# Turning the neighbourhood attention's probabilities: six TensorE transpositions a head replaced by VectorE block transpositions and a trip through DRAM

## The chip, the cores and the metric

The kernel runs on one core of one Trainium2 chip. The core has five engines that each work through their own instruction list in order and wait for one another by semaphores: TensorE (PE in the profile; PEld is its loading of stationary operands), VectorE (DVE), ScalarE (ACT), GpSimd (POOL) and SyncE (SP), which here issues nearly all transfers. The metric is device time in microseconds (us) of one launch, lower is better. A single core is used, so there is nothing to balance between cores.

## The reference, cut to what matters

The program is a two-layer encoder over 512 grid tokens and 16 learned "meta" tokens, 1024 features wide. In each layer one normalised input is projected to 42 chunks of 128 columns. They feed two attention branches and their gates; both branches are projected back, weighted by sigmoid gates, added and projected once more to the residual stream.

```python
# branch A: 8 query heads on 2 key heads, every query sees all 528 keys
p = softmax(q @ k.T * scale); o = p @ v
# branch B (neighbourhood): 8 heads, a grid query sees a window of 8 x 16 grid neighbours
# (with a learned bias) and the 16 meta keys; a meta query sees the meta keys alone
s_win  = einsum('bchd,bicjhd->bhcij', q_row, k_win) * scale + bias
s_meta = einsum('bchd,bmhd->bhcm', q_row, km) * scale
p = softmax(concat([s_win, s_meta])); o = p_win @ v_win + p_meta @ vm
```

All of it is float32. TensorE multiplies float32 values that were split into a high and a low part, and a product is the sum of three matmuls (high by high, high by low, low by high).

The second product of attention needs the probabilities with keys on the partitions (the 128 rows of on-chip memory), while the softmax leaves queries on them. So every block of probabilities has to be transposed between the two. That step is what the change is about.

## The kernel before, in words

The spine is `product` (line 316): one chunk of weights by all tokens. In layer 0 it runs two spans of 264 tokens with 24 matmuls each; in layer 1, where meta tokens are needed for keys and values alone, most chunks run one span of 512. Weights come in halves of 256 KB. `weights` (line 231) issues the load of a half on SP into one of four `raw` buffers, three halves ahead of their use; ScalarE then casts the high part (`whi`, line 240) and GpSimd subtracts the low part (`wlo`, line 241). So each weight load sits in SP's list among all other transfers, and a transfer that has to wait on SP holds up the weight loads behind it.

Attention is woven into the spine. After each span (and in the middle of a 512 span in layer 1) `tick` (line 310) is called, and two `Side` objects (line 279), one for each branch, run the parts that fall due. A unit of work starts every four ticks, and its parts have fixed numbers of ticks after the start: `GQA_AT` and `NA_AT` (lines 37 to 40). The neighbourhood branch starts one tick after the other (`GQA_AT_TICK, NA_AT_TICK`, line 44). A planner then orders each engine's list by the order in which the code was traced and its own estimates of readiness; parts under `high_priority` are drawn ahead.

`windowed_head` (line 967) is one head of the neighbourhood branch. Eight run in a layer. Its parts are:

- `prepare` (tick 0): SP loads the bias table (480 KB) into a `bias` tile of 960 columns; there are two such tiles.
- `scores` (tick 2): the queries are four tiles of 128, and each needs 208 or 272 keys (`BLK`, four column ranges of the bias tile). TensorE writes scores, VectorE adds the bias and takes the row maximum (line 990), ScalarE takes the exponential in place (line 992). In layer 0 there are 16 meta queries beside.
- `transposes1`, `transposes2`, `transposes3` (ticks 5, 5, 5 in layer 0; 4, 5, 5 in layer 1): nine TensorE transpositions (line 129, `transposed`) into three PSUM banks named `ta`, `tb`, `tc`: six of 128 by 128 probabilities, two of 80 columns (the tokens that only an edge tile needs with the meta keys), one of 64 columns around the meta keys. In layer 0 a fourth bank `tm` takes the meta queries. All come from the pool `ps_t`, which has two banks. `split` (line 191) empties a bank: ScalarE copies the high part (line 193), VectorE subtracts the low part (line 194). `split_meta` (line 784) does so for the meta keys.
- `sums` (tick 7): eleven matmuls with the values (line 1052) into one bank `avb`; then `combine` (line 765) and, after the second head of a pair, `gated` (line 775) write `ob`, the branch's output.

Beside them `divided_later` (line 800) sends the row sums of a pair of heads through DRAM and multiplies their inverse into the gate `zb` on GpSimd (line 822); it too has its transfers on SP. After the last head `side_na.finish()` runs all parts that are left with no ticks between, and the branch's output projection (`y<-ob`) follows.

Branch A (`global_unit`, line 847) already turns its probabilities another way, and its lines are a measure here: VectorE transposes within blocks of 32 by 32 in place (line 867), SP writes the tile to DRAM (line 870, `turn<-P`), reads it back in four transfers that put the blocks in their places (line 877, `P<-turn`), and `split` works from on-chip memory (`pth`, `ptl`).

## Time and profile before

| | |
|---|---|
| time, median of 3 runs | 853.73 us (852.26 to 855.82) |
| the profiled execution's own time | 855.46 us |
| its span, first to last instruction | 853.1 us |
| granted TensorE clock, mean | 0.992 |
| busy PE / PEld / DVE / ACT / POOL | 97% / 89% / 65% / 56% / 45% |
| neighbourhood heads run, layer 0 and layer 1 | about 84 to 256 us and 505 to 672 us |
| transfers | 135 MB in 113249 packets, mean 158 GB/s |

How to read it: the matmuls overlap, and a line's mean duration runs from its start to its modelled end, so the rate of the engine is read from the distance between starts. "Idle before" is time in which the engine stood still ahead of a group of instructions, and the arrow names what ended that time. The granted clock is 1.00 or 0.50 in any short stretch.

### The profile page before, as it was taken

To read this page: it belongs to the slowest core of one execution; us is meant where nothing else is said; L and a number is where in the kernel's file an instruction comes from. 1 tells how busy PE (TensorE), PEld (TensorE's weight loads), DVE (VectorE), ACT (ScalarE), POOL (GpSimd) and SP (SyncE) were. 2 spreads that over 40 slices of the span, in tenths; PEclk is the share of its full clock that TensorE was granted. 3 is DMA by queue.
4 is the path that set the end of the run, shared out by engine and by line. 5 is a ranking of instruction groups with operands and counts; after the bars stand their busy time and mean duration, and the time that the engine had idled before them with its cause. 6 is when DMAs were issued, how large, how long until landed. Compare 5 with 4: busy or idle time off the path is not lost.

```text
span 853.1 us, 16107 instructions
## 1 busy us (share of the span) xinstructions
PE 825.1 (97%) x5662; PEld 762.1 (89%) x5662; DVE 552.0 (65%) x1218; ACT 473.7 (56%) x1137; POOL 382.6 (45%) x296
## 2 busy tenths in 40 slices
PE   9999899989999999899999999999999999999997
PEld 9999899989999999899998989898987778878786
DVE  7976658777776675436447657777777657555633
ACT  8654677566764555333435456576757645543422
POOL 1663343343343333545765554443534433445851
PEclk9999999999999999999999999999999999999999
DMA  7277464566544564334555575657476655544502
GB/s 275 90 194 215 122 183 122 172 205 169 169 139 137 164 184 145 112 100 144 147 143 130 142 212 161 170 165 238 124 206 172 193 163 169 169 151 145 176 13 99
DMA packets 113249, 135.00 MB, mean 158 GB/s; under 512 B 31888, under 2 KB 66192, under 8 KB 113168
## 3 DMA queue, kind: packets, MB, share of 16 engines
q1 hardware_dynamic: 112448, 132.90, 53.0%
q8 instruction: 45, 0.74, 0.4%
q10 hardware_dynamic: 720, 1.06, 0.3%
q14 instruction: 36, 0.29, 0.1%
HBM read 98.50 MB, written 21.84 MB: 141 GB/s over the span
## 4 chain that ended last, share of the span: by engine, by line
PE 78%; DVE 8%; ACT 6%; issue 4%; DMA 2%; SPq 1%; POOL 1%; POOLq 0%; ACTq 0%; DVEq 0%
PE pp L327 16%; PE pp L325 16%; PE pp L326 16%; PE av L905 4%; PE y L327 3%; PE y L326 3%; PE y L325 3%; PE avb L1052 2%; DVE ptl L194 2%; PE pf L1234 2%; PE pf L1236 2%; PE pf L1235 2%; PE S L556 2%; PE S L557 1%; DVE ga L898 1%
## 5 line engine op out<-in xcount | busy, mean ns | idle before, releaser
L241 POOL TENSOR_TENSOR wlo<-raw,whi 128x512 fp32r<-128x512 f32 x210 | 289.2, 1386 | 404.7 <-ACT whi L240 325.0
L325 PE MATMUL pp<-hh,whi 128*128 128x264 f32 (+3 forms) x1040 | 326.6, 314 | 2.7 <-DVE mg L1131 1.5
L327 PE MATMUL pp<-hh,wlo 128*128 128x264 f32 (+3 forms) x1040 | 326.2, 314 | 1.3 <-POOL wlo L241 1.2
L326 PE MATMUL pp<-hl,whi 128*128 128x264 f32 (+3 forms) x1040 | 324.3, 312 | 0.0
L327 PEld LDWEIGHTS pp<-hh,wlo 128*128 128x128 f32 x1040 | 196.8, 189 | 12.9 <-POOL wlo L241 2.1
L325 PEld LDWEIGHTS pp<-hh,whi 128*128 128x128 f32 x1040 | 196.5, 189 | 12.4 <-DVE mg L1131 1.7
L326 PEld LDWEIGHTS pp<-hl,whi 128*128 128x128 f32 x1040 | 197.0, 189 | 9.5
L240 ACT CAST whi<-raw 128x512 fp32r<-128x512 f32 x210 | 127.6, 618 | 109.1 <-PE pp L326 41.1
L867 DVE STREAM_TRANSPOSE P<-P 128x512 f32<-128x512 f32 x64 | 46.4, 727 | 36.4 <-ACT P L841 35.7
L194 DVE TENSOR_TENSOR ptl<-P,pth 128x512 fp32r<-128x512 f32 x64 | 53.8, 841 | 5.4 <-ACT pth L193 4.7
L837 DVE CUSTOM_DVE_ANT_1 P<-S,r 128x528 f32<-128x528 f32 x64 | 44.9, 701 | 16.0 <-PE S L557 15.1
L1131 DVE TENSOR_TENSOR mg<-pp,rbc 128x264 f32<-128x264 f32 (+1 forms) x48 | 24.8, 517 | 39.0 <-PE pp L327 38.5
L841 ACT ACTIVATE P<-P,st 128x528 f32<-128x528 f32 x64 | 47.2, 737 | 1.9
L1132 ACT ACTIVATE mg<-mg 128x264 f32<-128x264 f32 (+1 forms) x48 | 23.7, 494 | 35.0 <-DVE mg L1131 34.8
L992 ACT ACTIVATE bias<-bias,stb 128x208 f32<-128x208 f32 (+1 forms) x64 | 31.0, 486 | 20.0 <-DVE stb L990 19.9
L193 ACT CAST pth<-P 128x512 fp32r<-128x512 f32 x64 | 39.3, 614 | 0.1
L840 ACT ACTIVATE st<-st 128x1 f32<-128x1 f32 x64 | 13.0, 203 | 45.4 <-DVE st L837 44.6
L905 PE MATMUL av<-ptl,VA 128*128 128x256 f32 x128 | 34.1, 294 | 3.3 <-DVE ptl L194 3.1
L326 PE MATMUL pp<-mx,whi 128*128 128x264 f32 x128 | 36.6, 286 | 0.0
L327 PE MATMUL pp<-mx,wlo 128*128 128x264 f32 x128 | 36.4, 284 | 0.0
L325 PE MATMUL pp<-mx,whi 128*128 128x264 f32 x128 | 36.3, 284 | 0.0
L905 PE MATMUL av<-pth,VA 128*128 128x256 f32 x128 | 34.8, 295 | 0.0
(534 smaller groups left out, 1731.6 us busy)
## 6 DMA issues: line engine op xcount, KB each, us to landing
raw<-in_w_dram SPq DMA_DIRECT2D x210, 256.0 KB
turn<-P SPq DMA_DIRECT2D x32, 528.0 KB
P<-turn SPq DMA_DIRECT2D x128, 128.0 KB
bias<-in_bias_dram SPq DMA_DIRECT2D x16, 480.0 KB
KB<-KB SPq DMA_DIRECT2D x24, 272.0 KB
rawl<-in_w_dram SPq DMA_DIRECT2D x16, 256.0 KB
x<-in_xT_dram SPq DMA_DIRECT2D x8, 264.0 KB
xr<-in_xT_dram SPq DMA_DIRECT2D x8, 264.0 KB
```

Of the source, the lines that this page charges most:

```text
L193: split_at["hi"] = nc.scalar.copy(hi, src)
L194: split_at["any"] = nc.vector.tensor_sub(lo, src, hi.bitcast(F32))
L240: cast = nc.scalar.copy(hi, raw)
L241: sub = nc.gpsimd.tensor_sub(lo, raw, hi.bitcast(F32))
L325: nc.tensor.matmul(ps, wh, rh[:, a:b], start=i == 0, stop=False)
L326: nc.tensor.matmul(ps, wh, rl[:, a:b], start=False, stop=False)
L327: nc.tensor.matmul(ps, wl, rh[:, a:b], start=False, stop=i == n - 1)
L837: newest["max"] = nc.vector.tensor_tensor_reduce(p[:n].rearrange("p (i k) -> p i k", i=2), S[:n, :, :HALF], scale[:n].unsqueeze(2).to_broa ...
L841: nc.scalar.activation(p[:n], p[:n], AF.Exp, bias=st[:n, 1:2], scale=1.0, accum_out=st[:n, 2:3] if total is None else total)
L867: nc.vector.transpose(c["both"][:n, a:b], c["both"][:n, a:b])
L905: nc.tensor.matmul(c["av"], rows2(c["t"][i][0]), c["t"][i][1], start=i == 0, stop=i == 8)
L992: nc.scalar.activation(pb[b], pb[b], AF.Exp, bias=st[:, b:b + 1], scale=-1.0, accum_out=total[:, b:b + 1])
```

## The change

The six full tiles of a head's probabilities (all 128 rows of the four query tiles, columns 80 to 464 and 496 to 880 of the bias tile) are no longer transposed by TensorE. The parts become:

- `turn` (tick 3): VectorE transposes the two column ranges of 384 in blocks of 32 by 32, in place, and one transfer writes both (384 KB) to a DRAM tile `turnedb`.
- `meta_turn` (tick 4, layer 0 alone): the meta queries' transposition, formerly in `transposes1`.
- `edges` (tick 4): the three transpositions that are left go into one bank `tb`; `split` on 80 by 256 and `split_meta` empty it.
- `back` (tick 4): four transfers of 96 KB read the blocks back into columns 0 to 768 of the same bias tile, each piece 32 values (128 bytes) long.
- `split_tiles` (tick 6): the high and low parts are made from the bias tile, a 128 by 512 and a 128 by 256 split.
- `sums` (tick 7): the same eleven matmuls in another order; the output bank holds the query tiles in the order 0, 2, 1, 3, and `combine` puts them right while adding.

The bias tile is now held until tick 6 rather than tick 5. The diff, cut to its core:

```diff
--- before.py
+++ after.py
@@ -36,8 +36,8 @@
 
 GQA_AT = ({"scores": (0, 1), "turn": (1, 2), "back": 3, "split": (5, 5), "ends": 5, "divide": (3, 4, 6), "sums": (7, 7)},
           {"scores": (0, 1), "turn": (1, 2), "back": 3, "split": (5, 5), "ends": 5, "divide": (3, 4, 6), "sums": (7, 7)})
-NA_AT = ({"stages": (0, 2, 5, 5, 5, 7), "values": (3, 4), "divide": (3, 4, 6)},
-         {"stages": (0, 2, 4, 5, 5, 7), "values": (3, 4), "divide": (3, 4, 6)})
+NA_AT = ({"stages": (0, 2, 3, 4, 4, 4, 6, 7), "values": (3, 4), "divide": (3, 4, 6)},
+         {"stages": (0, 2, 3, 4, 4, 6, 7), "values": (3, 4), "divide": (3, 4, 6)})
 
 NORM_AT = ({"tokens": (0, 1, 3), "squares": (1, 1, 2, 3, 2), "heads": (2, 3, 5, 7, 6), "values": (1, 4)},
            {"tokens": (1, 3, 5), "squares": (2, 2, 2, 3, 2), "heads": (2, 3, 5, 7, 6), "values": (1, 4)})
@@ -762,7 +762,7 @@
                 nc.vector.scalar_tensor_tensor(t[:, :N], th[:, :N], 1.0, t[:, :N], op0=ALU.add, op1=ALU.mult)
             return t
 
-        def combine(tag, o, hh, av, c0, n):
+        def combine(tag, o, hh, av, c0, n, order=lambda v: v):
 
             r, q = rows(hh)
             t = slot(tag, f"cmb{nc.next_id()}")
@@ -770,7 +770,7 @@
             with ExitStack() as held:
                 if "max" in newest:
                     held.enter_context(tc.issue_after(newest["max"].ins))
-                nc.vector.tensor_add(o[r, c0:c0 + n], av[r, :n], t[r, :n])
+                nc.vector.tensor_add(o[r, c0:c0 + n], order(av[r, :n]), order(t[r, :n]))
 
         def gated(tag, o, gate, name):
             hi, lo = two(tag, name, F32R)
@@ -964,6 +964,10 @@
 
         ob, kvq, zb = [None] * 4, {}, {}
 
+        def blocks(v):
+
+            return v.rearrange("p (x y q) -> p y x q", x=2, y=2)
+
         def windowed_head(hd):
 
             j, hh, nm = hd // 2, hd % 2, f"{l}_{hd}"
@@ -1004,55 +1008,68 @@
                     nc.scalar.mul(pm, pm, sm[:, 2:3])
                     c["pm"] = pw
 
-            def transposes1():
-                pb = c["p"]
-                tp = bank(ps_t, f"ta{nm}", "tp")
-                for i, (b, o0) in enumerate(((0, 80), (1, 16), (1, 144), (2, 0))):
-                    transposed(tp[:, P * i:P * (i + 1)], pb[b][:, o0:o0 + P])
-                c["a"] = slot("B", f"tah{nm}", F32R), slot("B", f"tal{nm}", F32R)
-                split(c["a"][0][:, :512], c["a"][1][:, :512], tp)
-                if full:
-                    ps = bank(ps_t, f"tm{nm}", "tp")[:32]
-                    transposed(ps[:, :P], c["pm"])
-                    ps = ps[:, :NMETA]
-                    mh = pad_tile("mm")
-                    nc.vector.tensor_copy(mh[:32], ps)
-                    nc.vector.tensor_sub(mh[64:96], ps, mh[:32].bitcast(F32))
-                    c["mt"] = mh
-
-            def transposes2():
+
+            def turn():
+                v = c["bias"][:, EDGE:EDGE + 832].rearrange("p (s x) -> p s x", s=2)[:, :, :3 * P]
+                for s in range(2):
+                    nc.vector.transpose(v[:, s], v[:, s])
+                c["there"] = dpool.tile([P, 6 * P], F32, tag="turnedb", bufs=3, name=f"turnb{nm}")
+                nc.sync.dma_start(c["there"].rearrange("p (s x) -> p s x", s=2), v)
+
+            def meta_turn():
+                ps = bank(ps_t, f"tm{nm}", "tp")[:32]
+                transposed(ps[:, :P], c["pm"])
+                ps = ps[:, :NMETA]
+                mh = pad_tile("mm")
+                nc.vector.tensor_copy(mh[:32], ps)
+                nc.vector.tensor_sub(mh[64:96], ps, mh[:32].bitcast(F32))
+                c["mt"] = mh
+
+            def edges():
+
                 pb = c["p"]
                 tp = bank(ps_t, f"tb{nm}", "tp")
-                transposed(tp[:, 0:P], pb[2][:, P:2 * P])
-                transposed(tp[:, P:2 * P], pb[3][:, 0:P])
-                transposed(tp[:EDGE, 2 * P:3 * P], pb[0][:, :EDGE])
-                transposed(tp[:EDGE, 3 * P:4 * P], pb[3][:, P:P + EDGE])
+                transposed(tp[:EDGE, :P], pb[0][:, :EDGE])
+                transposed(tp[:EDGE, P:2 * P], pb[3][:, P:P + EDGE])
+                transposed(tp[:64, 2 * P:3 * P], c["bias"][:, BLK_META:BLK_META + 64])
                 c["b"] = bh, bl = slot("B", f"tbh{nm}", F32R), slot("B", f"tbl{nm}", F32R)
-                split(bh[:, :256], bl[:, :256], tp[:, :256])
-                split(bh[:EDGE, 256:512], bl[:EDGE, 256:512], tp[:EDGE, 256:512])
-
-            def transposes3():
-                tp = bank(ps_t, f"tc{nm}", "tp")
-                transposed(tp[:64, :P], c["bias"][:, BLK_META:BLK_META + 64])
+                split(bh[:EDGE, 256:512], bl[:EDGE, 256:512], tp[:EDGE, :256])
 
                 c["m"] = tm = pad_tile("na")
-                split_meta([(tm[:, P:2 * P], tp[:, :P]), (tm[:, :P], tp[:, :P])], inner)
+                split_meta([(tm[:, :P], tp[:, 2 * P:3 * P]), (tm[:, P:2 * P], tp[:, 2 * P:3 * P])], inner)
+
+            def back():
+
+                there = c["there"].rearrange("(b j) (s x) -> j s b x", j=32, s=6)
+                for q in range(4):
+                    nc.sync.dma_start(c["bias"][32 * q:32 * q + 32, :6 * P].rearrange("j (s b i) -> j s b i", s=6, b=4),
+                                      there[:, :, :, 32 * q:32 * q + 32])
+
+            def split_tiles():
+                v = c["bias"][:, :6 * P].rearrange("p (s t x) -> p t s x", s=2, t=3)
+                c["a"] = slot("B", f"tah{nm}", F32R), slot("B", f"tal{nm}", F32R)
+                split(*(t[:, :512].rearrange("p (t s x) -> p t s x", t=2, s=2) for t in c["a"]), v[:, :2])
+                split(*(t[:, :256].rearrange("p (s x) -> p s x", s=2) for t in c["b"]), v[:, 2])
 
             def sums():
                 VB2, o = kvq[j]["v2"], kvq[j]["o"]
                 av = bank(ps_a, f"avb{nm}", "avn")
-                seq = [(5, c["m"], 0, 128, 384)]
+
+                cols = av.rearrange("p (x y q) -> p x y q", x=2, y=2)
+                seq = [(5, c["m"], 0, av[:, 128:384])]
+                for t in c["b"]:
+                    seq += [(3, t, 256, av[:, :128]), (4, t, 384, av[:, 384:])]
                 for t in c["a"]:
-                    seq += [(0, t, 0, 0, 256), (1, t, 256, 128, 384)]
+                    seq += [(0, t, 0, cols[:, :, 0]), (1, t, 256, av[:, 128:384])]
                 for t in c["b"]:
-                    seq += [(2, t, 0, 256, 512), (3, t, 256, 0, 128), (4, t, 384, 384, 512)]
-
-                for i, (u, t, c0, a, b) in enumerate(seq):
-                    r = slice(0, EDGE if u in (3, 4) else P)
-                    nc.tensor.matmul(av[:, a:b], rows2(VB2[r, u, hh]), t[r, c0:c0 + b - a], start=i == 0,
+                    seq += [(2, t, 0, cols[:, :, 1])]
+
+                for i, (u, t, c0, out) in enumerate(seq):
+                    r, n = slice(0, EDGE if u in (3, 4) else P), P if u in (3, 4) else 2 * P
+                    nc.tensor.matmul(out, rows2(VB2[r, u, hh]), t[r, c0:c0 + n], start=i == 0,
                                      stop=i == len(seq) - 1, skip_group_check=True)
                 def collect(av=av):
-                    combine("B", o, hh, av, 0, NREAL)
+                    combine("B", o, hh, av, 0, NREAL, blocks)
                     if full:
                         combine("B", o, hh, c["avm"], NREAL, NMETA)
                     if hh == 1:
@@ -1063,7 +1080,8 @@
                     nc.tensor.matmul(c["avm"], rows2(VB2[:, 5, hh]), c["mt"], start=True, stop=True)
                 ending.append(collect)
 
-            return prepare, scores, transposes1, transposes2, transposes3, sums
+            parts = [prepare, scores, turn, edges, back, split_tiles, sums]
+            return parts[:3] + ([meta_turn] if full else []) + parts[3:]
 
 
         stacks = {"next": 0, "scored": 0}
```

## The prediction

> **What bounds the kernel now.** I read the page's engine table first, then the chain that ended last, then the groups of instructions by shape, then two windows that hold the neighbourhood heads.
>
> ```profile
> span 853.1 us, 16107 instructions
> PE 825.1 (97%) x5662; PEld 762.1 (89%) x5662; DVE 552.0 (65%) x1218; ACT 473.7 (56%) x1137; POOL 382.6 (45%) x296
> PE 78%; DVE 8%; ACT 6%; issue 4%; DMA 2%; SPq 1%; POOL 1%; POOLq 0%; ACTq 0%; DVEq 0%
> 84.00:256.00 172.00, 163.42 (x1321) 160.58 (x1320) 124.44 (x348) 114.62 (x321) 66.97 (x52) 0.98 0.56 161
> 505.00:672.00 167.00, 162.12 (x1028) 144.10 (x1027) 125.91 (x300) 112.13 (x289) 69.76 (x51) 1.00 0.61 178
> ```
>
> TensorE is busy 97% of the span and is 78% of the chain, so a matmul taken away counts in full unless something else comes late. In the two windows (window, its length, then busy PE, PEld, DVE, ACT, POOL, the granted clock, share and rate of the transfers) VectorE is busy 250 of 339 us. PE stands idle 13.5 us there, and part of that is the step being changed:
>
> ```profile
> L129 PE MATMUL tb<-ident,bias 128*128 128x128 f32 x32 | 6.4, 281 | 4.7 <-DVE mm L1020 3.3 <-DVE tal L194 1.5
> L129 PE MATMUL tc<-ident,bias 128*64 128x128 f32 x16 | 4.5, 279 | 2.4 <-DVE mm L1020 2.0 <-DVE tal L194 0.4
> 98.49 0.63 PE L129 MATMUL tb<-ident,bias 128*128 128x128 f32 x4 [3.04 <-DVE mm L1020]
> 190.96 0.27 PE L129 MATMUL tc<-ident,bias 128*64 128x128 f32 x1 [2.03 <-DVE mm L1020]
> 99.50:102.90 3.40, 3.40 (x17) 3.40 (x16) 1.53 (x4) 1.09 (x4) 0.00 (x0) 0.50 0.71 233
> 191.60:195.00 3.40, 3.40 (x19) 3.37 (x19) 2.63 (x12) 1.45 (x6) 0.00 (x0) 0.50 0.54 142
> ```
>
> In one tick four banks are asked of a pool of two, and the third transposition stands until VectorE has emptied a bank. Those waits are 4.7 + 2.4 = 7.1 us in all. The two longest are each followed by a stretch of 3.4 us with the clock at 0.50, where the matmuls take twice as long: 1.7 us lost each.
>
> **The change part by part.** Durations come from the profiled execution, whose own time is 855.46 us (span 853.1 and 2.4 around it). That lies 1.73 above the median shown, 853.73, so I sum against 855.5 and take 1.7 off at the end.
>
> *Transpositions removed.* Six a head, 96 in all. Their mean of 272 ns is a latency; the rate is read from starts:
>
> ```profile
> 94.13 0.60 PE L129 MATMUL ta<-ident,bias 128*128 128x128 f32 x4
> 94.57 0.27 PE L129 MATMUL tm<-ident,pm 128*32 128x128 f32 x1
> ```
>
> Four take 94.57 - 94.13 = 0.44 us, 0.11 each: 96 x 0.11 = **-10.6 us**. The eleven matmuls of `sums` stay as they are.
>
> *Bank waits.* After the change a head asks for `tm` and `tb` in layer 0, and `tb` alone in layer 1, in one tick. On even heads `window_values` at tick 4 asks for a third, behind `tm`. I take 1.0 of the 7.1 as left: **-6.1 us** (bounds 0, if VectorE's lateness only moves the wait elsewhere, and -7.1). With the waits go the two slow stretches: **-3.4 us** (bounds 0 and -3.4).
>
> *VectorE, ScalarE, GpSimd.*
>
> ```profile
> L194 DVE TENSOR_TENSOR ptl<-P,pth 128x512 fp32r<-128x512 f32 x64 | 53.8, 841 | 5.4 <-ACT pth L193 4.7
> L194 DVE TENSOR_TENSOR tal<-ta,tah 128x512 fp32r<-128x512 f32 x16 | 10.9, 679 | 3.0 <-ACT tah L193 2.8
> L194 DVE TENSOR_TENSOR tbl<-tb,tbh 128x256 fp32r<-128x256 f32 x16 | 6.7, 418 | 1.9 <-ACT tbh L193 1.7
> L867 DVE STREAM_TRANSPOSE P<-P 128x512 f32<-128x512 f32 x32 | 22.7, 710 | 17.4 <-ACT P L841 17.1
> L193 ACT CAST pth<-P 128x512 fp32r<-128x512 f32 x64 | 39.3, 614 | 0.1
> L193 ACT CAST tah<-ta 128x512 fp32r<-128x512 f32 x16 | 9.3, 582 | 5.3 <-PE ta L129 5.2
> L241 POOL TENSOR_TENSOR wlo<-raw,whi 128x512 fp32r<-128x512 f32 x210 | 289.2, 1386 | 404.7 <-ACT whi L240 325.0 <-PE ta L129 14.1 <-PE tc L129 9.6
> ```
>
> Per head VectorE gains two block transpositions of 128x384 (no such row; between 710 x 384/512 = 0.53 and the full 0.71; 0.53 taken, since length sets most of it) and subtractions that now read on-chip memory (0.84, and half of it, 0.42, for 128x256). It sheds 0.68 and 0.42. Net 2 x 0.53 + 0.84 + 0.42 - 0.68 - 0.42 = +1.2 us, 20 us over 16 heads, which takes VectorE from 250 to 270 of 339 us. ScalarE's copies differ by 0.03. The sum takes **0** for both: PE's work covers them. If a fifth of the 20 us shows, it is 4.
>
> The rows show the on-chip subtraction at 841 ns against 679 with one operand in PSUM. The Trainium skill (SBUF — State Buffer, Who interferes with whom) gives a reason: a VectorE instruction with two operands in SBUF shares a read port with GpSimd, and one fully blocks the other. By that rule each head's new subtractions could hold up `wlo` by up to 1.3 us (estimate: 0.84 + 0.42), 20 us of blocking in all; the sum would move only as far as GpSimd's 404.7 us of idle time did not absorb it.
>
> *Transfers and SP.* Per head five more entries in SP's list. For their price I read branch A:
>
> ```profile
> 533.84 2.72 SPq L877 DMA_DIRECT2D P<-turn  x4
> 540.83 0.62 ACT L193 CAST pth<-P 128x512 fp32r<-128x512 f32 x1
> 608.66 0.33 SPq L870 DMA_DIRECT2D turn<-P  x1
> SPq L870 <- DVE P L867: 60.1, 16, 6.9
> SPq L877 <- DMA turn<-P: 28.4, 23, 3.6
> 404.13 1.60 SPq L1197 DMA_DIRECT2D x1d<-xt  x3
> 405.40:407.30 1.90, 1.90 (x17) 1.90 (x17) 0.00 (x0) 0.62 (x1) 0.51 (x1) 1.00 0.83 156
> ```
>
> Issue is 0.33 + 2.72 = 3.05 us a head. The wait of the write for VectorE is 60.1/16 = 3.8 us where there is one, the wait of the read for the write 28.4/23 = 1.2. Behind both stand weight loads. Pieces of 128 bytes: the only rows are the `x1d` stores, three of 64 KB in such pieces, in the 1.9 us window; so 384 KB take at most 2 x 1.9 = 3.8 us, most of it while the reads are still being issued; the transfer engines, at 0.56 and 0.61 in the two windows, have room for it.
>
> How much SP has to spare shows in layer 1:
>
> ```profile
> 599.72 2.44 SPq L235 DMA_DIRECT2D raw<-in_w_dram  x2
> 619.45 0.90 SPq L235 DMA_DIRECT2D raw<-in_w_dram  x2
> 627.08 0.50 PE L327 MATMUL pp<-hh,wlo 128*128 128x512 f32 x1 [0.71 <-POOL wlo L241]
> 643.13 0.50 PE L325 MATMUL pp<-hh,whi 128*128 128x512 f32 x1 [1.08 <-ACT whi L240]
> ```
>
> From 602.2 to 619.4 no weight load leaves SP, because it stands at branch A's turn and at other waits; 7.6 us after the late load PE stands still for it. So some of SP's new 8 us a head (3.05 + 3.8 + 1.2) reaches PE. Bounds 0, if it falls where loads are early, and 8 us in each of the two holes that already show, 16. Most loads are not that late, so I take **+4 us**.
>
> *The wait of `sums` for the trip.* From the last exponential: turn 1.1, write issued 0.3, landed and read back about 1.2 + 2.7 issue, landing 2 (the row at 540.83 bounds it by 4.3), split 0.61 + 0.84 + 0.42 = 1.9. Together 9.2 us. Today's room:
>
> ```profile
> 598.19 0.45 ACT L992 ACTIVATE bias<-bias,stb 128x208 f32<-128x208 f32 x1
> 611.51 0.28 PE L1052 MATMUL avb<-na,VB 128*128 128x256 f32 x1
> L905 PE MATMUL av<-ptl,VA 128*128 128x256 f32 x128 | 34.1, 294 | 3.3 <-DVE ptl L194 3.1
> ```
>
> 611.5 - 598.6 = 12.9 us, so it fits with 3.7 to spare if SP is on time. Branch A, with the same scheme, loses 3.3 us over 32 units in PE waits for `ptl`; for 16 heads with one tick less I take **+2 us** (0 to 10).
>
> *The last head of layer 1* has no ticks left to cover it:
>
> ```profile
> 662.18 0.45 ACT L992 ACTIVATE bias<-bias,stb 128x208 f32<-128x208 f32 x1
> 669.51 0.35 PE L1052 MATMUL avb<-na,VB 128*128 128x256 f32 x1
> 675.74 1.29 POOL L822 TENSOR_TENSOR zb<-zb,sumsb 128x512 f32<-128x512 f32 x1
> 678.60 0.50 PE L325 MATMUL pp<-hh,whi 128*128 128x512 f32 x1 [1.53 <-DVE mg L1131]
> ```
>
> Exponentials to `sums` is 6.9 us today and 9.2 after. The gate `zb` is behind SP too: its read of the row sums comes after the four reads of `back`, 2.7 us. PE already waits at the end, so I take **+3 us** (0 to 8).
>
> *Sum.* -10.6 - 6.1 - 3.4 + 4 + 2 + 3 = -11.1. 855.5 - 11.1 = 844.4; less 1.7, **843 us**. The first three terms are the gain, 20.1, and the last three are what comes back, 9.
>
> **The rivals.**
> B, *nothing comes back*: SP's delays fall where weight loads are early. For it: the `wlo` row's 325 us of idle time behind `whi`, so weights are mostly ahead. Against it: the two stops at 627 and 643. 853.7 - 20.1 = 833.6; with the bounds of the small terms 831 to 837.
>
> C, *the trip is late for `sums`*. If a piece of 128 bytes costs as much as one of branch A's 512 bytes, then the 3072 pieces of a head take 3 times as long as the 1024 of the four reads at 533.84: with the 2.72 us in which those are issued, 8.2 us rather than 3.8. Then the trip is 13.6 us against 12.9, and every wait on SP shows. Eight heads of layer 1 at 1.5 us and three slow stretches of 1.7 are 17; the gain less that and the +3 at the end is 0: about 853. The Trainium skill (DMA: Bandwidth & Descriptors, Specifications) speaks for it: transfers in pieces under 512 bytes don't reach full rate. The `x1d` row speaks against so high a price, but those are stores, and these are loads.
>
> D, *SP holds the weights back*, slower. Place: weight loads behind the new write and read, in layer 1 from 560 to 650 us. Price: 8 us a head wholly exposed, and 1.7 for the slow clock after it, 9.7. It decides from two such heads on (19.4 against 20.1 gained). With three, 29 - 20 = +9: 863 us. For it: the hole at 602. Against it: SP's list has 221 us of waiting for free `raw` buffers, which shrinks before PE feels anything:
>
> ```profile
> SPq L235 <- POOL wlo L241: 221.0, 113, 7.9
> ```
>
> That the change does not do what it says would be the bank waits staying elsewhere: 9.5 of the gain gone, 853, an outcome like C's.
>
> **How the numbers follow.** The forecast (837 to 849) 0.40, B 0.18, C with the case just named 0.21, D 0.21. About 0.5%, 4.3 us, is what a measurement of this kernel can tell from no change: faster is below 849.5, slower above 858. Faster 0.40 + 0.18 = 0.58, same 0.21, slower 0.21. The range goes from B's 831 into the mild part of D, 860; outside lie about 0.03 below and 0.17 above. The forecast's own range is 837 to 849, from terms of +2 to +15 coming back instead of 9.
>
> **What would show it.** The `tb` and `tc` rows with waits of VectorE gone, x48 transpositions instead of x144, and no clock of 0.50 near 100 and 192 us: the gain. PE waits for `wlo` and `whi` over 2.7 us in all, or `raw` rows with gaps of more than 17 us: SP's term too small. A PE wait at `avb` on the new splits, or ScalarE idle behind a transfer of `turnedb`: the trip is late. A wait at the end of layer 1 above 1.5 us: the last term. I am wrong if PE's busy time doesn't fall by some 10 us, or if it does and its idle time rises by as much.

## The result and the profile after

The changed kernel takes 930.0 us (median, 927.87 to 934.53) where the kernel before takes 854.12 us beside it (852.26 to 855.82). The ratio is 1.090, with a 95% interval of 1.085 to 1.094. The prediction said 843 us, and faster; it was slower by 76 us, outside the range. All times from here on are medians of fast runs; two far slower ones (4509.51 us of `trip_act`, 1333.48 us of the kernel before) are left out.

The head of the page of the changed kernel (span; busy time of each engine, its share and its instructions) and its chain of waits:

```profile
span 929.5 us, 16071 instructions
...
PE 853.4 (92%) x5566; PEld 776.2 (84%) x5566; DVE 563.0 (61%) x1250; ACT 474.8 (51%) x1137; POOL 379.4 (41%) x296
...
PE 62%; DVE 9%; DMA 9%; SPq 7%; ACT 6%; issue 5%; POOL 2%; POOLq 0%; ACTq 0%; DVEq 0%
```

TensorE has 96 matmuls fewer, and it is busy 28.3 us longer (825.1 before, 853.4 after). It also stands still 48.1 us longer (853.1 - 825.1 = 28.0 before, 929.5 - 853.4 = 76.1 after). That is the whole 76.4 us of the span. It is busy longer because its clock is lower: the mean granted clock is 0.957 after and 0.992 before, so the share of the span that the clock did not grant is 929.5 x 0.043 = 40.0 us against 853.1 x 0.008 = 6.8 us, 33.2 us more. Against this stand the removed transpositions, some 10 us; about 6 us of the busy time stay unassigned.

The groups of TensorE's instructions in the changed kernel (count, busy, mean ns, then the idle time ahead of the group and what ended it), with VectorE's block transposition and GpSimd's `wlo`:

```profile
L129 PE MATMUL tb<-ident,bias 128*80 128x128 f32 (+1 forms) x48 | 10.7, 293 | 1.5 <-ACT bias L996 0.9 <-ACT st L840 0.6
L129 PE MATMUL tm<-ident,pm 128*32 128x128 f32 x8 | 2.2, 276 | 3.8 <-DVE VB L194 3.8
L325 PE MATMUL pp<-hh,whi 128*128 128x264 f32 (+3 forms) x1040 | 335.1, 322 | 22.0 <-ACT whi L240 21.3 <-DVE mg L1149 0.8
L327 PE MATMUL pp<-hh,wlo 128*128 128x264 f32 (+3 forms) x1040 | 335.0, 323 | 7.7 <-POOL wlo L241 7.6
L1069 PE MATMUL avb<-tah,VB 128*128 128x256 f32 x32 | 7.2, 308 | 3.2 <-ACT tah L193 3.2
L1015 DVE STREAM_TRANSPOSE bias<-bias 128x384 f32<-128x384 f32 x32 | 17.3, 563 | 7.2 <-ACT bias L996 7.1
L241 POOL TENSOR_TENSOR wlo<-raw,whi 128x512 fp32r<-128x512 f32 x210 | 284.9, 1367 | 442.1 <-ACT whi L240 382.9 <-PE avb L1069 14.5 <-DMA raw<-in_w_dram 14.1
```

The 48 transpositions that remain are there, and the waits behind `mm` and `tal` at `tb` and `tc` are gone, as the prediction asked. But `tm`, which takes a bank of the same pool of two, now waits 3.8 us for `VB`, whose split empties such a bank; before, `tm` waited for nothing. New is the wait for weights: 21.3 us behind `whi` and 7.6 us behind `wlo`. In the kernel before these two waits (what TensorE waits to start, for whom; us in total, times, longest) were:

```profile
PE pp L327 <- POOL wlo L241: 1.2, 2, 0.7
PE pp L325 <- ACT whi L240: 1.1, 1, 1.1
```

One such wait, in the timeline of SP and TensorE (start, length, engine, line, transfer or matmul; in brackets the idle time before it):

```profile
142.21 1.26 SPq L235 DMA_DIRECT2D raw<-in_w_dram  x2
...
152.96 0.64 SPq L1017 DMA_DIRECT2D turnb<-bias  x1
166.32 0.61 SPq L811 DMA_DIRECT2D thereb<-invb  x2
...
170.05 1.38 SPq L235 DMA_DIRECT2D raw<-in_w_dram  x2
173.87 0.59 PE L325 MATMUL pp<-hh,whi 128*128 128x264 f32 x1 [6.13 <-ACT whi L240]
```

The slow stretch that begins within this wait, as a window (the clock stands behind GpSimd's busy time):

```profile
170.90:181.10 10.20, 6.68 (x29) 6.38 (x30) 0.87 (x2) 1.82 (x4) 3.81 (x3) 0.50 0.72 174
```

For 27 us no weight load leaves SP. It stands from 153.6 to 166.3 at the row sums (`thereb`), which wait for VectorE. TensorE then waits 6.1 us, from 167.7 to 173.9, and the clock is at 0.50 for 10.2 us, from 170.9 on. This looks like rival D. The experiments show that the trip's own entries are not needed for it.

### The profile page after: what moved, and what is told of

Its sections match the earlier page's. It is cut to its first block, busy times and chain, and to the rows that moved or that the text cites. A ratio compares the mean times of both kernels' runs of the same rounds, so it can differ in the third digit from the quotient of the medians.

```text
span 929.5 us, 16071 instructions
## 1 busy us (share of the span) xinstructions
PE 853.4 (92%) x5566; PEld 776.2 (84%) x5566; DVE 563.0 (61%) x1250; ACT 474.8 (51%) x1137; POOL 379.4 (41%) x296
## 4 chain that ended last, share of the span: by engine, by line
PE 62%; DVE 9%; DMA 9%; SPq 7%; ACT 6%; issue 5%; POOL 2%; POOLq 0%; ACTq 0%; DVEq 0%
PE pp L327 14%; PE pp L325 13%; PE pp L326 13%; PE y L325 3%; PE y L327 3%; PE y L326 3%; PE av L905 2%; DMA raw<-in_w_dram 2%; DVE ptl L194 2%; SPq L877 2%; POOL wlo L241 2%; DMA KB<-KB 2%; PE pf L1254 1%; PE pf L1252 1%; PE pf L1253 1%
## 5 line engine op out<-in xcount | busy, mean ns | idle before, releaser
L241 POOL TENSOR_TENSOR wlo<-raw,whi 128x512 fp32r<-128x512 f32 x210 | 284.9, 1367 | 442.1 <-ACT whi L240 382.9
L325 PE MATMUL pp<-hh,whi 128*128 128x264 f32 (+3 forms) x1040 | 335.1, 322 | 22.0 <-ACT whi L240 21.3
L327 PE MATMUL pp<-hh,wlo 128*128 128x264 f32 (+3 forms) x1040 | 335.0, 323 | 7.7 <-POOL wlo L241 7.6
L326 PE MATMUL pp<-hl,whi 128*128 128x264 f32 (+3 forms) x1040 | 330.2, 318 | 0.0
L325 PEld LDWEIGHTS pp<-hh,whi 128*128 128x128 f32 x1040 | 203.5, 196 | 34.5 <-ACT whi L240 24.5
L327 PEld LDWEIGHTS pp<-hh,wlo 128*128 128x128 f32 x1040 | 203.1, 196 | 24.5 <-POOL wlo L241 13.6
L326 PEld LDWEIGHTS pp<-hl,whi 128*128 128x128 f32 x1040 | 203.4, 196 | 9.5
L194 DVE TENSOR_TENSOR ptl<-P,pth 128x512 fp32r<-128x512 f32 x64 | 49.5, 782 | 8.5 <-ACT pth L193 6.6
L325 PE MATMUL y<-ob,whi 128*128 128x264 f32 (+1 forms) x96 | 31.8, 333 | 5.2 <-DVE mg L1149 2.8
```

Source lines behind the costliest of these rows:

```text
L194: split_at["any"] = nc.vector.tensor_sub(lo, src, hi.bitcast(F32))
L241: sub = nc.gpsimd.tensor_sub(lo, raw, hi.bitcast(F32))
L325: nc.tensor.matmul(ps, wh, rh[:, a:b], start=i == 0, stop=False)
L326: nc.tensor.matmul(ps, wh, rl[:, a:b], start=False, stop=False)
L327: nc.tensor.matmul(ps, wl, rh[:, a:b], start=False, stop=i == n - 1)
```

## The experiments

The theories are these. S: SP works its list in order, so the trip's entries hold the weight loads back, and the clock halves after the stops. P, later T: the traffic, pieces of 128 bytes above all, is slow. V: VectorE's new work takes the gain. L, a wider S: whatever stands behind the trip in any list is late. O, which came last: the planner, told of other transfers, puts the instructions of all engines in another order, and that order is the cost.

### The trip, its size and its time

`no_trip` is the changed kernel without the write and the four reads, so the blocks stay in the wrong places.

```diff
-                nc.sync.dma_start(c["there"].rearrange("p (s x) -> p s x", s=2), v)
...
-                for q in range(4):
-                    nc.sync.dma_start(c["bias"][32 * q:32 * q + 32, :6 * P].rearrange("j (s b i) -> j s b i", s=6, b=4),
-                                      there[:, :, :, 32 * q:32 * q + 32])
```

> The changed kernel without its two transfer steps: the block transpositions stay, the write to DRAM and the four reads back are left out, and the split reads the tile as it lies (so the blocks of the probabilities stand in wrong places; part of the computation, the moving of blocks, is left out). Theory S (SyncE's list holds the weight loads back, and each stop of TensorE over 2 us halves its clock afterwards): the loss of 76 us goes with the trip, time 830 to 845, as in the gain terms of the prediction (853.7 - 20 = 834). Theory V (VectorE's extra work, or another order of the engines' lists, makes TensorE late): stays above 900. Theory P (the 128-byte pieces are slow): also 830 to 845; the next run tells S and P apart.

852.93 us, ratio 0.999 (0.996 to 1.001). The loss goes with the trip, but no gain is left. As for VectorE, its busy time is 572.3 us here, 20.3 more than before, as the prediction worked out.

`before_trip` is the kernel before with the same five transfers a head beside it, into a bias tile that nothing reads afterwards:

```diff
-            return prepare, scores, transposes1, transposes2, transposes3, sums
+            return prepare, scores, sent, transposes1, transposes2, transposes3, returned, sums
```

Here `sent` (tick 3) is the write and `returned` (tick 6) the four reads.

> The kernel before with the trip added and its data not used: after the exponentials the 384 KB are written to DRAM (tick 3), and after the transpositions the four reads bring them back into the bias tile, which is dead by then (tick 6). Theory S: the trip alone costs most of the loss, 895 to 930. Theory V: 853 to 865, since TensorE, VectorE and ScalarE do what they did before.

927.66 us, ratio 1.085 (1.077 to 1.093). So the loss comes with the trip alone, without any of the other edits. Whether it is the transfers on the chip or what the planner makes of them, this run cannot tell.

`big_pieces` reads the same bytes in rows of 3 KB, so that the blocks are not moved to their places:

```diff
-                there = c["there"].rearrange("(b j) (s x) -> j s b x", j=32, s=6)
+                flat = c["there"].rearrange("(q j) x -> q j x", j=32)
...
-                    nc.sync.dma_start(c["bias"][32 * q:32 * q + 32, :6 * P].rearrange("j (s b i) -> j s b i", s=6, b=4),
-                                      there[:, :, :, 32 * q:32 * q + 32])
+                    nc.sync.dma_start(c["bias"][32 * q:32 * q + 32, :6 * P], flat[q])
```

> The changed kernel with the four reads back taken as whole rows of 3 KB instead of 128-byte pieces: as many bytes and as many entries in SyncE's list, the blocks of the probabilities are not put in their places (that part of the computation is left out). Theory S: little changes, 915 to 935 against 930. Theory P (piece size): back to 850 or below.

896.36 us, ratio 1.049 (1.042 to 1.056): between what S and P asked. One read is issued in 0.44 us rather than 0.67.

`before_tiny` is `before_trip` with the five entries and a twelfth of the bytes:

```diff
-                nc.sync.dma_start(c["there"].rearrange("p (s x) -> p s x", s=2), v)
+                nc.sync.dma_start(c["there"].rearrange("p (s x) -> p s x", s=2), v[:, :, :32])
...
+                    nc.sync.dma_start(c["bias"][32 * q:32 * q + 32, :64], there[32 * q:32 * q + 32])
```

> The kernel before with the unused trip of before_trip (927.66 us), at the same ticks and with the same five entries in SP's list and the same waits, but a twelfth of the bytes: one write of 128 by 64 and four reads of 32 rows of 256 bytes. What stays is the order and the waits; what goes is the issue time of many pieces and their time in the transfer engines. Theory S with waits as the main part: 890 to 930. Theory T, and S with issue time as the main part: 855 to 875.

873.13 us, ratio 1.023 (1.017 to 1.030): below what S asked of the waits, at the upper end of T.

`send_later` puts the write into a part of its own, `send`, a tick later, and the reads, splits and sums one tick later too:

```diff
-            parts = [prepare, scores, turn, edges, back, split_tiles, sums]
+            parts = [prepare, scores, turn, send, edges, back, split_tiles, sums]
```

> The changed kernel with the write to DRAM issued one tick after the block transpositions (tick 4), the reads at tick 5, the split at 7 and the sums at 8, nothing else changed. In the changed kernel SyncE waits some 49 us for the transposition ahead of the write. Theory S with the waits as its cause: most of these 49 us go, and the time falls to 870 to 900. Theory S with the issue time as its cause (5 entries, 3 us a head) or theory P: no change, 920 to 935.

944.48 us, ratio 1.105 (1.098 to 1.112), outside both ranges. More time for the write's wait did not help in this form; the lists came out in another order here too.

Up to here the size seemed to matter. A direct reading speaks against T: from the issue of a weight load to the end of its last packet, over the 210 loads of each trace:

```
                     median   mean
before               2.53     2.73 us
after                2.66     2.85
before_trip          2.58     2.83
```

The loads are issued late; once issued they land 0.1 us later than before.

### Other queues

`before_raw_pool` and `raw_pool` give the weight loads to GpSimd's queue in the kernel before and after, `before_raw_act` and `raw_act` to ScalarE's (`nc.scalar`), and `trip_act` gives the trip's five transfers to ScalarE:

```diff
-            nc.sync.dma_start(raw, w[l_, c_][:, 4 * P * i:4 * P * (i + 1)])
+            nc.gpsimd.dma_start(raw, w[l_, c_][:, 4 * P * i:4 * P * (i + 1)])
```

> The kernel before with the same edit alone: weight loads issued by GpSimd. It prices the edit without the trip. Theory S: the holes in SP's list that the kernel before already shows cost it little (2.7 us of PE waits), so 845 to 856. If GpSimd's issuing is dear for wlo, over 860, and raw_pool has to be read against this run rather than against the kernel before.

> The changed kernel, trip and all, with one edit: the weight loads (line 235) are issued by GpSimd instead of SP, so that no transfer of the trip stands ahead of them in a list. Theory S (the weights come late because SP's list is worked in order, and the clock halves after the stops): most of the 76 us comes back, 850 to 870, weight-load gaps of 20 us and more are gone, half-clock stretches fall from 81 us to under 30. Theory T (the trip's traffic itself, 128-byte pieces in the transfer engines, slows the weight loads): the loads still take longer to land and the time stays above 900. If GpSimd's issuing is itself dear (it makes wlo), PE waits for wlo grow and the time lies between.

> The kernel before with the weight loads (line 235) issued by ScalarE, on a queue of the same kind as SP's, so that they cost no more to issue but stand in ScalarE's list. It prices that edit alone; ScalarE then carries some 75 us of issue more. Theory S: 850 to 870. GpSimd's issuing cost 33 us (before_raw_pool, 888.76); if this costs as much, then the order of the lists that the new queue brings is the price, not the engine.

> The changed kernel with the weight loads on ScalarE's queue, the trip alone on SP. In raw_pool (GpSimd's queue) PE's waits for whi and wlo were gone, yet the trip still cost 86 us against before_raw_pool, with PE behind VectorE. Theory S in its narrow form (weight loads behind the trip in SP's list): within 15 us of before_raw_act. Theory L (whatever an in-order list holds behind the trip is late: on SP the key and query copies and branch A's transfers, on ScalarE and VectorE what stands behind the two splits): over 40 us above before_raw_act, with PE waiting for VectorE and ScalarE and not for whi and wlo.

> The changed kernel with the trip's five transfers issued by ScalarE, the weight loads on SP as before. SP's list is then that of the kernel before. Theory S: 850 to 880, with PE's waits for whi and wlo back to some 5 us, unless ScalarE, which makes whi, stands itself at the trip's waits. Theory L: ScalarE now holds whi behind the write's wait for VectorE and the read's wait for the write, so over 900, with PE behind ACT.

```
loads on       kernel before                     changed kernel
GpSimd         888.76 us, 1.041 (1.037-1.045)    974.84 us, 1.140 (1.134-1.145)
ScalarE        897.67 us, 1.051 (1.047-1.054)    997.91 us, 1.168 (1.164-1.171)
trip on ScalarE                                  919.17 us, 1.078 (1.073-1.083)
```

With the loads off SP the change costs 86 and 100 us, not less than 76. With the trip off SP it still costs some 65, where S asked for 850 to 880 us in all. TensorE's longest waits in `raw_act` (what it waits to start, for whom; us in total, times, longest):

```profile
PE avb L1069 <- DVE na L798: 18.4, 5, 6.4
PE av L905 <- DVE ptl L194: 10.8, 18, 2.2
PE av L905 <- ACT pth L193: 8.8, 12, 3.4
PE pp L325 <- DVE za L756: 8.3, 3, 6.3
```

The weights are no longer waited for, and the time is worse. S in its narrow form falls. L foretold this, but these runs cannot show L either: with each new queue all lists come out in another order, and the kernel before lost 33 and 44 us by that edit alone.

### The gain alone

`spread` asks for the bank waits without the trip: bank `tc` one tick later in the kernel before.

```diff
-NA_AT = ({"stages": (0, 2, 5, 5, 5, 7), "values": (3, 4), "divide": (3, 4, 6)},
-         {"stages": (0, 2, 4, 5, 5, 7), "values": (3, 4), "divide": (3, 4, 6)})
+NA_AT = ({"stages": (0, 2, 5, 5, 6, 7), "values": (3, 4), "divide": (3, 4, 6)},
+         {"stages": (0, 2, 4, 5, 6, 7), "values": (3, 4), "divide": (3, 4, 6)})
```

> The kernel before with the third group of transpositions (bank tc) one tick later, 6 instead of 5, in both layers; nothing else. It asks for the bank waits alone (7.1 us, and 3.4 us of slow clock after them), with all transpositions kept. If they can be had by moving them: 843 to 850. If VectorE's lateness only moves the wait elsewhere, as no_trip suggests (852.93 us with 96 transpositions fewer): 852 to 857.

854.05 us, ratio 0.999 (0.997 to 1.001). Its groups for the two banks:

```profile
L129 PE MATMUL tb<-ident,bias 128*128 128x128 f32 (+1 forms) x64 | 9.8, 276 | 5.7 <-DVE mm L1020 4.4 <-DVE tal L194 1.1
...
L129 PE MATMUL tc<-ident,bias 128*64 128x128 f32 x16 | 4.4, 276 | 0.8 <-DVE tal L194 0.8
```

The wait of `tc` fell from 2.4 to 0.8 us and that of `tb` rose from 4.7 to 5.7, so most of the 7.1 us only moved. The longest stop, 3.04 us ahead of `tb`, is the same as in the kernel before, but no slow stretch follows it here (the stop, then a window behind it):

```profile
98.73 0.63 PE L129 MATMUL tb<-ident,bias 128*128 128x128 f32 x4 [3.04 <-DVE mm L1020]
98.70:105.00 6.30, 6.27 (x54) 6.30 (x55) 4.15 (x17) 2.74 (x10) 0.00 (x0) 1.00 0.56 179
```

So the 3.4 us that the prediction set down for two slow stretches do not belong to the waits as such; the last section has what decides.

`no_turn` is `no_trip` without VectorE's block transpositions too:

```diff
-                for s in range(2):
-                    nc.vector.transpose(v[:, s], v[:, s])
```

> no_trip (852.93 us) without VectorE's two block transpositions a head as well, so that 96 of PE's transpositions are gone and VectorE has some 17 us less to do than in no_trip. It leaves the turning of the probabilities out. Theory V (VectorE's lateness took the gain of the removed transpositions): 838 to 847. If the gain isn't there even so: 850 to 855, and what the transpositions cost on PE was room that something else had filled.

851.74 us, ratio 0.997 (0.994 to 0.999). The busy times of `no_turn`, then two waits of TensorE in it:

```profile
PE 818.8 (96%) x5566; PEld 754.4 (89%) x5566; DVE 555.7 (65%) x1218; ACT 473.6 (56%) x1137; POOL 381.2 (45%) x296
```

```profile
PE avb L1062 <- DVE na L798: 4.2, 3, 2.2
PE vtc L739 <- DVE na L798: 3.1, 2, 2.3
```

In `no_turn` the waits at `tb` are all but gone (0.3 us) and there is no `tc`, and in their place TensorE waits 4.2 + 3.1 = 7.3 us for VectorE's `na`, against 1.1 us in the kernel before. The 3.1 at `vtc` are a wait for a bank of the same pool. TensorE is busy 6.3 us less; at a clock of 0.987 some 4 us of the 10.6 saved are lost again. VectorE's block transpositions, the one edit between `no_turn` and `no_trip`, cost about 1 us (852.93 and 851.74), no more than the runs of one kernel differ. So V falls too: the gain is not there even without them. One doubt stays: the lists of `no_turn` are not those of the kernel before either (57 of the 210 casts `whi` and 55 of the 128 products `av<-ptl` stand at another place among the instructions that both have). No run removes the transpositions and holds the rest, so it isn't shown whether the gain was never there or was lost to the order.

### The order of the lists

The planner writes every engine's list from its own estimates. In the kernel before and in `before_trip` the computing engines have the same instructions, but not in the same order. Comparing the places of each instruction in the two lists:

```
engine    instructions   at another place     mean of all and largest move, in places
ScalarE   whi<-raw       89 of 210            2.9 later, up to 25 later
TensorE   S<-KA1h,Q      27 of 64             17.9 earlier, up to 138 earlier
TensorE   av<-ptl,VA     72 of 128            5.2 later, up to 38 later
```

So attention's scores come earlier and the casts of weights later. Six kernels hold the order. Each chains every engine's instructions, in the places that a list recorded from another kernel gives, without adding a wait between them; in the traces of the five whose source kernel was run, every list stands exactly in the order asked for:

```diff
+    for engine, places in HELD.items():
+        row = [by[engine][k] for k in places]
+        for a, b in zip(row, row[1:]):
+            tc.add_manual_dep(b, a.name, mybir.DependencyInfo(mybir.DependencyClass.NoSync, mybir.DependencyReason.DATA),
+                              reason="held")
```

`order_before`: the kernel before, no trip, in the order of `before_trip`.

> The kernel before, without any trip, but with every engine's list held to the order that before_trip has (927.66 us); nothing is added or left out. Theory S (the trip's entries and transfers cost the time on the chip): the order alone costs little, 850 to 865. Theory O (the planner, told of 80 more transfers, puts the instructions of all engines in a worse order, and that is the cost): most of the 72 us is here, 900 to 930.

931.84 us, ratio 1.090 (1.085 to 1.094). The order alone costs all of it, 76 us, and a little more than O's range. TensorE's longest waits in `before_trip`, which has the trip, and in `order_before`, which has none (the lines of the second lie 4 further down):

```profile
PE pp L325 <- ACT whi L240: 15.0, 8, 7.3
PE pp L327 <- POOL wlo L241: 8.8, 15, 1.8
PE av L905 <- ACT pth L193: 7.8, 6, 2.4
```

```profile
PE pp L329 <- ACT whi L244: 14.3, 8, 6.4
PE pp L331 <- POOL wlo L245: 8.9, 14, 1.7
PE av L909 <- ACT pth L197: 7.8, 6, 2.4
```

```profile
SPq L815 <- DVE invb L813: 68.3, 6, 24.9
```

They are the same waits, and as the last row, from SP's waits in `order_before`, says, SP stands up to 24.9 us at the row sums with no trip in its list.

`order_no_trip`: `no_trip` in the order of the changed kernel.

> no_trip (852.93 us) with every engine's list held to the order of the changed kernel (930.0 us); the trip is still left out, so the probabilities are not turned whole. Theory S: 850 to 865. Theory O: 900 to 930, that is, the changed kernel's time without its trip.

928.3 us, ratio 1.086 (1.081 to 1.091), where `no_trip` in its own order takes 852.93. Its two longest waits of TensorE, and the hole in its SP's timeline, to be laid beside those of the changed kernel above:

```profile
PE pp L329 <- ACT whi L244: 21.8, 12, 7.3
PE pp L331 <- POOL wlo L245: 7.0, 14, 0.8
```

```profile
152.90 1.15 SPq L539 DMA_DIRECT2D KB<-KB  x2
167.38 0.61 SPq L815 DMA_DIRECT2D thereb<-invb  x2
...
171.12 1.06 SPq L239 DMA_DIRECT2D raw<-in_w_dram  x2
```

The hole stands at the same place, within 1.1 us, although nothing of the trip is there. The changed kernel itself takes 930.0, so in these lists the trip adds nothing that can be measured.

`held_before_trip`: the trip of `before_trip`, put between SP's entries, with everything else in the order of the kernel before.

> The kernel before with the unused trip of before_trip at full size, but with every engine's list held to the order of the kernel before; the 80 entries of the trip are put between SP's, and nothing else differs. Theory S: 900 to 930. Theory O: 853 to 870, at most what SP's 63 us of issue and its waits push onto weight loads.

893.34 us, ratio 1.047 (1.042 to 1.051): above O's 853 to 870, below S's 900 to 930, so it fits neither. The trip in lists that were not made for it costs 38 us, half of what the order costs. TensorE's longest waits are for attention here, and `whi` is not among them:

```profile
PE tb L133 <- DVE mm L1035: 5.9, 3, 3.0
PE av L909 <- ACT pth L197: 5.1, 2, 4.4
PE S L560 <- DVE st L841: 4.6, 2, 2.3
```

`order_compute`: `order_before` with SP's list as in the kernel before.

> order_before (931.84 us, no trip) with SP's list put back to the order of the kernel before; the lists of TensorE, VectorE, ScalarE and GpSimd stay in the order that before_trip has. If the cost sits in SP's order (weight loads placed behind entries that wait for VectorE): 855 to 875. If it sits in the lists of the computing engines: 915 to 940.

941.99 us, ratio 1.101 (1.097 to 1.106). The cost sits in the lists of the computing engines: it stays when SP's order is put back. What SP's order would cost alone, with the other lists as before, no run asks.

`A_in_big`: the changed kernel, with its pieces of 128 bytes, in the order of `big_pieces`.

> The changed kernel as it is, with its reads in pieces of 128 bytes, but with every engine's list held to the order of big_pieces (896.36 us). Theory O (big_pieces was faster because the planner, told of cheaper reads, ordered the lists better): 890 to 905. Theory P (pieces of 128 bytes cost time on the chip, in SP's issue and in the transfer engines): 920 to 935, as the changed kernel.

900.67 us, ratio 1.053 (1.050 to 1.056). Of the 34 us between the changed kernel and `big_pieces` 29 are the order and 4 are left for the pieces. No run holds a kernel to its own order, so these 4 us contain whatever the holding itself costs; unless small pieces save time, it is not more.

`A_in_tiny`: the changed kernel, complete, in an order made for a twelfth of the trip's bytes.

> The changed kernel as it is, with every engine's list held to an order that the planner made for the same work and the same dependences, but with the trip's transfers shown to it as a twelfth of their bytes. Theory O: the less the planner is told of the trip, the nearer the lists are to those of the kernel before, and the nearer the time comes to held_before_trip (893.34 us) or below: 870 to 900. If the planner's order had been right for the chip: 930 or more. Faster than the kernel before it would only be if the trip cost nothing: below 853.

884.41 us, ratio 1.034 (1.031 to 1.036). The same work and transfers, 46 us faster than the changed kernel by order alone. It is the best of the kernels with a trip at full size; no kernel that does all the work was faster than the one before by more than can be measured.

What stays open: which of the moved instructions cost most, what the planner believes of a transfer, and how much of its 31 us over the kernel before `A_in_tiny` owes to the trip and how much to its order. That a larger trip makes it move more is read from the order alone: lists made for the trip at a twelfth, in 3 KB pieces and as it is give the changed kernel 884, 901 and 930 us. The changed kernel in lists made without any trip was not tried.

## Why the prediction was wrong

*What bounds the kernel.* "A matmul taken away counts in full unless something else comes late": something did. 96 transpositions less gave 0.3% (`no_turn`), 2 to 3 us, in lists that were not quite the same.

*Transpositions removed* (-10.6) is right as work: 6.3 us less busy time in `no_turn` and some 4 us given to the slower clock. But it is not a term of the end: 2.5 us more idle time and the clock took most of it.

*Bank waits* and the slow stretches (-6.1, -3.4) failed. The waits went from their rows as foretold, and came back elsewhere: at `tm` in the changed kernel, at `na` and `vtc` in `no_turn`. The bound of 0, "if VectorE's lateness only moves the wait elsewhere", is what the runs show. In `spread` they moved between the banks; its ten executions have a mean clock of 0.996 against 0.994 beside it, some 2 us, and the time does not differ by more than can be measured. That each long wait brings a slow stretch was luck of its place in time: in `spread` the same stop of 3.04 us brought none.

*VectorE, ScalarE, GpSimd* (0) held. The block transposition takes 0.563 us (0.53 taken), the subtractions from on-chip memory 0.77 and 0.55 (0.84 and 0.42); VectorE grows by 11 us, not 20; in `no_trip`, at the old pace, it does grow by 20. GpSimd was not held up on the whole: `wlo` takes 1367 ns after and 1386 before. But the two engines do meet. In the changed kernel's trace the 45 `ptl` subtractions with no GpSimd instruction beside them take 683 ns in the mean and 695 at most, the 19 others 1014 and up to 1789; alone, an on-chip subtraction is as fast as one from PSUM (679). This agrees with the rule of the Trainium skill (SBUF — State Buffer, Who interferes with whom) that a VectorE instruction with two operands in SBUF contends with GpSimd's reads.

*Transfers and SP* (+4, bounds 0 to 16) is the step that failed most, twice over. Its size: in lists made without it the trip costs 38 us (`held_before_trip`), more than twice the upper bound of 16, which counted the two holes that already showed. Its kind: the sum laid the new entries on a list that otherwise stays as it is, although a planner writes the lists. The planner reorders all five lists, and that reordering costs 76 us with no transfer in it, while the trip in lists made for it adds nothing (927.66 with, 931.84 without).

*The wait of `sums`* (+2, 0 to 10): the splits are waited for 3.2 us at `tah`, and some 3 us at `tal` and `tbl`; within its bounds, but not for its reason. `order_no_trip`, which has no trip to wait for, waits 2.8 us at `tah` and 1.8 at `tal`, and ScalarE's cast `tah` stands behind the trip's reads for 1.4 us in all.

*The last head* (+3, 0 to 8): TensorE waits 4.4 us and 2.4 us at the end of layer 1, where one wait of 1.5 stood, 5.3 more, and the clock is at 0.50 for the 13.7 us from 744.3 to 758.0, which takes another 6.8. Together that is over the bound. And it is not the trip: the same two stops, of the changed kernel first, stand in `order_no_trip`:

```profile
745.08 0.58 PE L905 MATMUL av<-pth,VA 128*128 128x256 f32 x1 [4.41 <-ACT pth L193]
752.43 0.80 PE L325 MATMUL y<-ob,whi 128*128 128x512 f32 x1 [2.42 <-ACT ob L193]
```

```profile
741.52 0.38 PE L909 MATMUL av<-pth,VA 128*128 128x256 f32 x1 [4.01 <-ACT pth L197]
748.59 0.79 PE L329 MATMUL y<-ob,whi 128*128 128x512 f32 x1 [2.41 <-ACT ob L197]
```

*Rivals.* B needed a gain that no run shows. C, the late trip, is hardly seen (1.4 us at `tah`); its price for small pieces, and with it the rule of the Trainium skill (DMA: Bandwidth & Descriptors, Specifications) on transfers under 512 bytes, is worth 4 us at most here (`A_in_big` against `big_pieces`). D had the sign and the picture right, weights late and then a slow clock, and asked for three heads; the rows show it in more places. But its cause, the trip's entries ahead of the weight loads, is not what makes it: the same holes stand in `order_no_trip`. That the order of the lists could change was in neither the sum nor the rivals.

*What would show it.* The sign named for being wrong came: TensorE's busy time rose by 28.3 us instead of falling by 10. So did the one named for SP, waits for `whi` and `wlo` over 2.7 us and gaps between weight loads over 17 us: 28.9 us and 27 us. Read without the held orders it would have confirmed the wrong cause.

## What to carry to other kernels

Where a planner writes the lists, an edit has two prices, its own and that of the order it brings. They come apart with two kernels: the old work in the new order, and the new work (here the old work and the trip) in the old order. Until the first has run, a wait in the new profile is no evidence that the edit's own instructions cause it.

A TensorE at 97% does not promise that work taken from it comes off the end; a kernel with that work simply left out gives a first answer in one run, before anything is built in its place, and a second one, with the other instructions held in their order, would settle it.

## What the runs showed of the hardware

The clock follows a fixed grid. In each of the 20 traces all stretches at 0.50 begin on a grid of 3.413 us, within 1 ns. Idle time is counted from the modelled ends of the matmuls. Sorting the windows of that grid by how long TensorE stood still in them:

```
TensorE idle in a window    next window at 0.50, if this one is
(of 3.413 us)               at full clock         at 0.50
0 to 0.5 us                 0 of 4268             14 of 189
0.5 to 0.8                  0 of 189              16 of 17
0.8 to 1.4                  11 of 253             37 of 37
1.4 to 2.0                  73 of 123             18 of 18
over 2.0                    92 of 92              35 of 35
```

At full clock about half a window of idle time halves the next one; at half clock half a microsecond is enough to stay there. Several short waits cost as much as a long one: of the 123 windows in the fourth row, the 31 with no single stop of 1.0 us or more in them were followed by a halved one in 25 cases. A long stop that the grid cuts in two may cost nothing: the 3.04 us of `spread` lie in two windows, with 1.69 and 1.35 us, and the same stop in the kernel before has 2.4 us in one window. And a stop in a slow stretch prolongs it. This fits with the 33 us of lost clock that came with 48 us of new idle time. The Trainium skill (TensorE: Matmul & The Clock Gate, What's actually happening) has the free-running window of 3413 ns, which the traces bear out, and the low clock after at least one idle window; here a window that was idle for 2.0 of its 3.4 us was enough each time.
